# Split norm sums and gate, a reordered GDN chain and a smaller weight ring in the projection stage of a hybrid GDN / RWKV-7 block

## The chip, the cores and the metric

The kernel runs on one core of a Trainium2 chip. The metric is the device time of one launch in microseconds (us), lower is better. The five engines are named as in the profile: PE is TensorE, DVE is VectorE, ACT is ScalarE, POOL is GpSimd, SP is the queue that issues most DMAs.

## The reference

One layer on x of 512 tokens by 2048 features, all in fp32, with a memory of 256 tokens:

```python
xn = RMSNorm(h);  y = xn @ W_in            # columns for 8 GDN heads x 128 and 16 RWKV heads x 64
h += concat[GDN(y_gdn), RWKV7(y_rwkv)] @ W_out
h += CrossAttn(RMSNorm(h), RMSNorm(mem))   # 4 heads of 512 into the 256 memory tokens
h += SquaredReLU_MLP(RMSNorm(h))           # hidden 8192
out = RMSNorm_final(h)

# GDN, per head: q, k, v = silu(causal conv of 4 taps); z gates the output
q = l2norm(q) * 128 ** -0.5;  k = l2norm(k)
# per chunk: M = strict(kb k^T * gamma), solve (M + 1) [U, W] = [v*b, kb*exp(G)]
v_new = U - W @ S;  o = qd @ S + (q k^T * gamma) @ v_new;  S = S * exp(gl) + kt^T @ v_new
out = rmsnorm(o) * norm_w * silu(z)
# RWKV-7, per head: S_t = S_{t-1} (diag(w_t) + a_t b_t^T) + v_t k_t^T, o_t = S_t r_t,
# with a norm of the keys, a group norm of o over 64 channels, a bonus term (r*k summed) * v,
# and an output gate sigmoid(y_g1) @ g2 of rank 160
```

## The kernel before

Features lie on partitions and the 512 tokens on the free axis, so a product of one weight block is 128x128 times 128x512. Weights and activations are split into two f32r parts (hi and lo), and each product of fp32 operands is made as three: hi·hi, hi·lo and lo·hi. For weights a half tile of 128x1024 (512 KB) is read into a raw buffer `wraw`; ACT casts it to `whi`, DVE subtracts to get `wlo`. The raw ring has `NWR` = 3 buffers in the pool `pw`, `whi` and `wlo` have two each (`NWS`). A few products stay plain fp32, among them the sums over channels that the norms need (a product with a constant matrix: `ones`, or `bones`, which is ones in the two 64x64 blocks on the diagonal) and RWKV's output gate (`pgt`).

The program has two parts. The first, up to about 1211 us, is ordered by hand. Generators yield one operation at a time; `run()` estimates for each waiting operation when it could start, issues the earliest, and keeps a model clock of each engine. `TE`, `DV`, `AC`, `GS` and `SY` are the lanes of the engines and of SP; `SL` is SP with an added wait for what it stores. `after(...)` holds a generator until an event. All these operations have one line in the profile, L249. In this part run:

- `projections()`: 59 tiles py of the input projection (16 steps of 3 products each), then kp (keys of the memory, 16 tiles of two halves with 16 products each) and kq (32 halves of 24 products with 256 columns). For each head pair the tiles are r, k, v of RWKV and then q, k, v, z of one GDN head. `evict` and `qevict` take results out of PSUM into one of `NY` = 6 buffers `ybuf`; `qevict` then stores 256 KB to `KQd` (kqd) in DRAM.
- `loader()`: splits weight halves and refills the raw ring through `rawload`.
- `rwkv(j)` and `gdn(h)`, eight chains each: convolutions or token shifts, norms, products within the chunk, the inverse of a triangular matrix (`inverse_blocks` on GpSimd for 16x16 blocks, then levels on TensorE), and a scan over chunks (products `rs` and `gs`). Their results go to `mixd` (mx when read back).

In a GDN chain the three convolutions come first, then both norm sums (`gn`), then the products of keys with keys (`pkk`) and queries with keys (`pqk`), and then the inverse starts. Further norm sums are `gon` (output of GDN), and `pn`, `pb`, `pvr` (keys, bonus and group norm of RWKV). Temporaries of 128x512 come from small rings: `sr` (2), `st` (2), `sg` (3).

The second part is written in plain order; a tile framework sets its waits. It begins when the pools of the first part (`pm`, `pq`) are closed and a pool `pl` is opened in their place: the results in `mixd` are read back and split (`oh`, `ol`), vp makes the values of the memory from `wv` (line L125 for its products, L133/L134 for the split, L153 for the weight load), then vo, op, sc, at, up and dn follow. The pool `pw` with the raw ring stays open over both parts.

Of the kernel before, what the change touches and what calls it, by code (L numbers as in the profile page):

```python
# [27 lines left out]
for _n, _w in (("ident", 128), ("ones", 128), ("bones", 128), ("mA", 128),  # L28
               ("lv64", 2 * 64), ("cen", 64), ("sneg", 128), ("mbias", 128),
               ("rst64", 512)):  # L30
    CST[_n] = (_off, _w)
    _off += _w
# [13 lines left out]
def constants():  # L46
    c = np.zeros((P, NCST), np.float32)

    def put(name, a):
        o, w = CST[name]  # L50
        c[:, o:o + w] = a
# [4 lines left out]
    put("bones", (i[:, None] // 64 == i[None, :] // 64))  # L56
# [18 lines left out]
def build(tc, I, out):  # L75
# [9 lines left out]

    pq_cm = tc.tile_pool(name="pq", bufs=1)
# [22 lines left out]
    ident, ones, bones = K("ident"), K("ones"), K("bones")  # L109
# [30 lines left out]
    NWR, NWS, NY = 3, 2, 6  # L140
    wcnt = [0]

    def wraw():
        wcnt[0] += 1
        return tile_of(pw, [P, 1024], F32, "wraw", f"wraw{wcnt[0]}", NWR)
# [128 lines left out]
    def after(*ev):  # L274
        return lambda: ev in events
# [50 lines left out]

    def act_tile(nm, dt=F32R):
        return tile_of(pa, [P, 512], dt, "act", nm, 32)
# [16 lines left out]
    NSH = {"sr": 2, "st": 2, "sg": 3}  # L345
# [78 lines left out]
    dp = pq.tile([P, 149], F32, name="dp")  # L424
    omu = dp[:, 0:27]
    hw0, ha0, hka = dp[:, 27:35], dp[:, 35:43], dp[:, 43:51]
    hgnw = dp[:, 148:149]
    hconv = dp[:, 51:147]
    nA = dp[:, 147:148]

    def derived():
        yield DV.tensor_scalar(out=omu, in0=cols("mu"), scalar1=-1.0, scalar2=1.0, op0=ALU.mult, op1=ALU.add)
        for o, n in ((hw0, "w0"), (ha0, "a0"), (hka, "ka"), (hgnw, "gnw"), (hconv, "conv")):
            yield DV.tensor_scalar(out=o, in0=cols(n), scalar1=0.5, scalar2=None, op0=ALU.mult)
# [123 lines left out]
    sg1 = pq.tile([P, T], F32, name="sg1")  # L558
    y2 = pq.tile([P, T], F32, name="y2")
# [3 lines left out]
    def rows():  # L563
# [13 lines left out]
        yield AC.activation(wa[0:64, :], wa[0:64, :], AF.Tanh)  # L577
        yield from shiftmix(1, 1, sg1)
        yield AC.activation(sg1, sg1, AF.Tanh, scale=0.5)
        yield DV.tensor_scalar(out=sg1, in0=sg1, scalar1=0.5, scalar2=0.5, op0=ALU.mult, op1=ALU.add)  # L580
        events.add(("lowrank",))
# [5 lines left out]
        x_, e_ = short(t="st"), short(t="st")  # L587
# [11 lines left out]
        tail = short(t="st")  # L599
# [43 lines left out]
    def inverse_blocks(nm, store, m, tags, sh, out):  # L643
# [5 lines left out]
        s1, s2 = short(512, sh), short(512, sh)  # L649
        q = lambda a: a[0:np_].rearrange("p (a b) -> p a b", b=16)  # L650
        D, Td, Ud = q(s1[:, 0:256]), q(s1[:, 256:512]), q(s2[:, 0:256])
# [3 lines left out]
        for j in range(15):  # L655
            w = 15 - j
            t = s2[0:np_, 256:256 + w * (j + 1)].rearrange("p (a b) -> p a b", b=j + 1)
            yield GS.tensor_tensor(out=t, in0=D[:, j, j + 1:16].unsqueeze(2).broadcast_to([np_, w, j + 1]),
                                   in1=Td[:, j:j + 1, 0:j + 1].broadcast_to([np_, w, j + 1]), op=ALU.mult)
            yield GS.tensor_tensor(out=Td[:, j + 1:16, 0:j + 1], in0=Td[:, j + 1:16, 0:j + 1], in1=t, op=ALU.add)  # L660
        yield GS.tensor_copy(Ud, Td.rearrange("p a b -> p b a"))
        Tm, Tt = (tl(t)[:, 0:m * 32].rearrange("p (c t) -> p c t", t=64) for t in tags[1:])
# [40 lines left out]
    def rwkv(j):  # L703
        base = 3 + 7 * j
        js = slice(j * P, (j + 1) * P)
        lw, lg = tl("lw", P), tl("lg", 2 * P, 2)
        yield SY.dma_start(lw, I["w2a2"][:, js])
        yield SY.dma_start(lg[:, 0:P], I["g2a"][:, js])
        yield SY.dma_start(lg[0:32, P:2 * P], I["g2b"][:, js])
# [23 lines left out]
        yield TE.matmul(pn, bones, sq, start=True, stop=True)  # L733
# [44 lines left out]
        chain(inverse_blocks(f"ri{j}", store, 16, ("k", "r", "E2"), "sr", inv), 1, ("ri", j))  # L778
        yield DV.scalar_tensor_tensor(out=kp, in0=r_, scalar=col("rk", j), in1=kp, op0=ALU.mult, op1=ALU.mult)
        pb = psb(f"pb{j}")  # L780
        yield TE.matmul(pb, bones, kp, start=True, stop=True)
# [47 lines left out]
        yield AC.copy(ov, pov)  # L829
        yield after("ri", j)  # L830
# [13 lines left out]
        if j < 7:  # L844
            chain(rwkv(j + 1), 3)

# [27 lines left out]
        sq = short(t="st")  # L874
        yield AC.activation(sq, cen, AF.Square)
        pvr = psb(f"pvr{j}", "scr", 1)
        yield TE.matmul(pvr, bones, sq, start=True, stop=True)
# [11 lines left out]
    def gdn(h):  # L889
        base = 3 + 7 * h + 3  # L890
        gsh = lambda w=512: short(w, "sg")
        yield after("rows")
# [4 lines left out]
        silu = []  # L897
        for s in range(3):
            yield after("py", base + s)
            y = ybuf[ys[base + s]]  # L900
            a = gsh()
            cv = lambda i: hconv[:, (s * 8 + h) * 4 + i:(s * 8 + h) * 4 + i + 1]
            yield AC.activation(a, y[:, 0:512], AF.Copy, scale=cv(0))
            for i in range(1, 4):
                yield DV.scalar_tensor_tensor(out=a, in0=y[:, i:i + 512], scalar=cv(i), in1=a,
                                              op0=ALU.mult, op1=ALU.add)
            yfree.append(ys.pop(base + s))
            t = gsh()
            yield AC.activation(t, a, AF.Tanh)
            o = tl(("gq", "gk", "gv")[s])  # L910
            yield DV.scalar_tensor_tensor(out=o, in0=t, scalar=1.0, in1=a, op0=ALU.add, op1=ALU.mult)
            silu.append(o)
        q_, k_, v_ = silu
# [7 lines left out]

        c3 = lambda a: a.rearrange("p (c t) -> p c t", t=P)
        sqs = []
        for x in (k_, q_):
            sq = gsh()
            yield AC.activation(sq, x, AF.Square)
            pn = psb(f"gn{h}_{len(sqs)}", "mg")
            yield TE.matmul(pn, ones, sq, start=True, stop=True)
            sqs.append((sq, pn))
        for c in range(4):  # L930
            cs = slice(c * P, (c + 1) * P)
            if c == 0:
                EG = tl("gEG")
                yield AC.activation(EG, E, AF.Exp)
                eg = tl("eg", 4, 2)
                yield DV.tensor_copy(eg.unsqueeze(2), c3(EG)[:, :, P - 1:P])
            yield DV.scalar_tensor_tensor(out=E[:, cs], in0=E[:, cs], scalar=RT[:, c, 0, h:h + 1],
                                          in1=K("mbias"), op0=ALU.subtract, op1=ALU.min)
        yield AC.activation(E, E, AF.Exp)
        Es = tl("gEs")  # L940
        yield GS.tensor_tensor(out=c3(Es), in0=c3(E), in1=K("sneg").unsqueeze(1).broadcast_to([P, 4, P]), op=ALU.mult)
        nrm = []
        for (sq, pn), x, bias, tag in ((sqs[0], k_, None, "gkn"), (sqs[1], q_, b_lq, "gqn")):
            yield from rsq_(sq, pn, 1.0, b_eps6, bias)
            xn = tl(tag)
            yield DV.tensor_tensor(out=xn, in0=x, in1=sq, op=ALU.mult)
            nrm.append(xn)
        kn, qn = nrm
        kb = tl("gk")
        yield DV.tensor_tensor(out=kb, in0=kn, in1=B, op=ALU.mult)  # L950
        pkk = psb(f"pkk{h}", "mg")
        for c in range(4):
            cs = slice(c * P, (c + 1) * P)
            yield TE.matmul(pkk[:, cs], kn[:, cs], kb[:, cs], start=True, stop=True)
        wd, qd = tl("gq"), B
        yield DV.tensor_tensor(out=wd, in0=kb, in1=EG, op=ALU.mult)
        yield DV.tensor_tensor(out=qd, in0=qn, in1=EG, op=ALU.mult)
        NTm = tl("gEG")
        yield DV.tensor_tensor(out=NTm, in0=pkk, in1=Es, op=ALU.mult)

        def store(full):
            yield SY.dma_start(full[:, 0:4, :], c3(NTm)[hA, :, 0:64])
            yield SY.dma_start(full[:, 4:8, :], c3(NTm)[hB, :, 64:128])

        inv = []
        pqk = psb(f"pqk{h}", "mg")
        for c in range(4):
            cs = slice(c * P, (c + 1) * P)
            yield TE.matmul(pqk[:, cs], kn[:, cs], qn[:, cs], start=True, stop=True)
        pkt = psb(f"pkt{h}", "mg")  # L970
        for c in range(4):
            cs = slice(c * P, (c + 1) * P)
            yield TE.transpose(pkt[:, cs], kn[:, cs], ident)
        Aq = tl("gAq")
        yield DV.tensor_tensor(out=Aq, in0=pqk, in1=E, op=ALU.mult)
        chain(inverse_blocks(f"gi{h}", store, 8, ("gkn", "gk", "gqn"), "sg", inv), 1, ("gi", h))
        pvt = psb(f"pvt{h}", "mg")
        for c in range(4):
            cs = slice(c * P, (c + 1) * P)
            yield TE.transpose(pvt[:, cs], v_[:, cs], ident)  # L980
        vb, kt = tl("gv"), tl("gkt")
        yield DV.tensor_tensor(out=c3(kt), in0=c3(pkt), in1=RT[:, :, 2, h:h + 1].broadcast_to([P, 4, P]), op=ALU.mult)
# [386 lines left out]
```

## Time and profile before

| | |
|---|---|
| median of 3 runs | 3179.08 us (3178.40 to 3180.32) |
| profiled execution | 3178.97 us |
| its span in the profile | 3177.1 us |
| granted TensorE clock, mean | 0.997 |
| TensorE busy | 3127.4 us |
| DVE, ACT, POOL busy | 1527.5, 1153.6, 195.5 us |
| stages by start of their products | py from 10 us, kp from 994, kq from 1106, vp from 1211, up and dn from 1757 |

A row of the profile names line, engine and operation, then output <- inputs with buffer numbers left out, and the number of instructions. A plain fp32 product shows as two matmul records. The chain of waits is followed back from the last instruction; "issue" in it is time in which the engine waited for nothing that is recorded. Recorded durations of pipelined matmuls overlap, so what one costs TensorE is read from the distance between starts.

### The profile page before, as it was taken

Reading aid. Unit: us, or ns where it says so; the run is one execution under the profiler, and the core shown is the slowest. Engines: PE = TensorE matmul, PEld = TensorE weight load, DVE = VectorE, ACT = ScalarE, POOL = GpSimd, SP = SyncE. Lnnn points to the kernel's source line nnn. Section 1 sums busy time; section 2 is a strip of 40 time slices with the busy share of each in tenths; the row PEclk is TensorE's granted clock in tenths of the full one; section 3 lists DMA queues with packets and bytes.
Section 4 is the critical chain, followed back from the end, with each engine's and each line's share of the span. In section 5 each row is a group of like instructions: output and inputs, shape, how many; then the busy total and the mean of one; then the engine's idle time right before and its main releaser. Section 6 shows DMA issues by size and latency. Waiting matters only on the chain.

```text
span 3177.1 us, 44277 instructions
## 1 busy us (share of the span) xinstructions
PE 3127.4 (98%) x18294; PEld 2552.0 (80%) x18294; DVE 1527.5 (48%) x2157; ACT 1153.6 (36%) x1468; POOL 195.5 (6%) x549
## 2 busy tenths in 40 slices
PE   8999999999999999999999999999999999999997
PEld 6777777777778798878878888888888888888885
DVE  6555566565566646534336433333343333333344
ACT  5435344354355555543324322222221222222222
POOL 0121120220220200000000000000000000000000
PEclk9999999999999999999999999999999999999998
DMA  5322322322424577663323222222222223222222
GB/s 177 88 76 84 89 81 77 98 81 76 124 82 140 160 231 258 227 226 126 109 93 93 94 98 97 96 100 93 100 94 99 99 94 100 93 99 96 96 100 93
DMA packets 202363, 360.57 MB, mean 113 GB/s; under 512 B 88553, under 2 KB 107757, under 8 KB 202161
## 3 DMA queue, kind: packets, MB, share of 16 engines
q1 hardware_dynamic: 197552, 349.35, 34.7%
q10 hardware_dynamic: 4608, 8.39, 0.7%
q8 instruction: 144, 2.36, 0.3%
q14 instruction: 59, 0.48, 0.0%
HBM read 326.86 MB, written 30.81 MB: 113 GB/s over the span
## 4 chain that ended last, share of the span: by engine, by line
PE 95%; DMA 2%; ACT 1%; DVE 1%; issue 0%; SPq 0%; ACTq 0%; DVEq 0%
PE dn L125 22%; PE up L125 22%; PE py L249 21%; PE op L125 5%; PE sc L125 3%; PE kq L249 3%; PE at L125 3%; PE kp L249 2%; PE vo L125 2%; PE vp L125 2%; PE gs L249 1%; PE rs L249 1%; DMA mx<-mixd 1%; PE pgA L249 1%; PE po L249 0%; PE gn L249 0%
## 5 line engine op out<-in xcount | busy, mean ns | idle before, releaser
L133 ACT CAST whi<-wraw 128x1024 fp32r<-128x1024 f32 x368 | 387.1, 1052 | 1101.1 <-PE dn L125 471.3
L134 DVE TENSOR_TENSOR wlo<-wraw,whi 128x1024 fp32r<-128x1024 f32 x368 | 451.1, 1226 | 536.0 <-ACT whi L133 534.9
L125 PE MATMUL dn<-ul,whi 128*128 128x512 f32 x1024 | 399.3, 390 | 0.0
L125 PE MATMUL up<-nl,whi 128*128 128x512 f32 x1024 | 398.7, 389 | 0.0
L125 PE MATMUL dn<-uh,wlo 128*128 128x512 f32 x1024 | 398.4, 389 | 0.0
L125 PE MATMUL dn<-uh,whi 128*128 128x512 f32 x1024 | 398.4, 389 | 0.0
L125 PE MATMUL up<-nh,wlo 128*128 128x512 f32 x1024 | 398.3, 389 | 0.0
L125 PE MATMUL up<-nh,whi 128*128 128x512 f32 x1024 | 398.3, 389 | 0.0
L249 PE MATMUL py<-xhi,whi 128*128 128x512 f32 x928 | 377.2, 406 | 10.8 <-ACT xhi L249 10.3
L249 PE MATMUL py<-xlo,whi 128*128 128x512 f32 x928 | 379.2, 409 | 0.1
L249 PE MATMUL py<-xhi,wlo 128*128 128x512 f32 x928 | 375.1, 404 | 0.0
L249 DVE TENSOR_TENSOR wlo<-wraw,whi 128x1024 fp32r<-128x1024 f32 x180 | 221.3, 1230 | 145.8 <-ACT whi L249 135.6
L249 ACT CAST whi<-wraw 128x1024 fp32r<-128x1024 f32 x180 | 188.9, 1049 | 271.9 <-PE py L249 215.4
L1263 DVE TENSOR_TENSOR h<-h,dn 128x512 f32<-128x512 f32 x128 | 88.1, 688 | 400.1 <-PE dn L125 400.1
L125 PEld LDWEIGHTS dn<-ul,whi 128*128 128x128 f32 x1024 | 192.2, 188 | 42.6 <-DVE ul L134 2.9
L125 PEld LDWEIGHTS up<-nh,wlo 128*128 128x128 f32 x1024 | 192.2, 188 | 40.3 <-issue 0.2
L125 PEld LDWEIGHTS up<-nl,whi 128*128 128x128 f32 x1024 | 192.2, 188 | 40.1 <-issue 0.2
L125 PEld LDWEIGHTS dn<-uh,wlo 128*128 128x128 f32 x1024 | 192.2, 188 | 40.0
L125 PEld LDWEIGHTS dn<-uh,whi 128*128 128x128 f32 x1024 | 192.2, 188 | 39.7
L125 PEld LDWEIGHTS up<-nh,whi 128*128 128x128 f32 x1024 | 192.2, 188 | 39.7
L249 PEld LDWEIGHTS py<-xhi,whi 128*128 128x128 f32 x928 | 175.4, 189 | 52.7 <-ACT xhi L249 10.3
L249 PEld LDWEIGHTS py<-xlo,whi 128*128 128x128 f32 x928 | 175.3, 189 | 41.4 <-issue 5.8
(558 smaller groups left out, 4710.2 us busy)
## 6 DMA issues: line engine op xcount, KB each, us to landing
wraw<-in_w_up SPq DMA_DIRECT2D x128, 512.0 KB, 3.5
wraw<-in_w_dn SPq DMA_DIRECT2D x128, 512.0 KB, 3.6
wraw<-in_w_in SPq DMA_DIRECT2D x118, 512.0 KB, 3.8
wraw<-in_wk SPq DMA_DIRECT2D x32, 512.0 KB, 3.8
wraw<-in_wqT SPq DMA_DIRECT2D x32, 512.0 KB, 4.2
wraw<-in_wv SPq DMA_DIRECT2D x32, 512.0 KB, 3.7
wraw<-in_wo SPq DMA_DIRECT2D x32, 512.0 KB, 4.2
wraw<-in_w_out SPq DMA_DIRECT2D x32, 512.0 KB, 3.7
```

The lines of the kernel that those rows point to most:

```text
L125: PE.matmul(o, l, r, start=start, stop=stop)
L133: S.copy(hi, src)
L134: V.tensor_tensor(out=lo, in0=src, in1=hi.bitcast(F32), op=ALU.subtract)
L249: f(*a, **k)
L1263: V.tensor_tensor(out=hres[n], in0=hres[n], in1=pt, op=ALU.add)
```

## The change

- GDN chain: the key's convolution comes first, then its norm, `pkk`, and the start of the inverse with temporaries of its own (`sgi`, `sgj`; the matrix in `gN`); then query, value and z. The inverse's last steps wait for the event `gq`. The columns of W_in are laid out as k, q, v, z for this.
- `sums_`: each of the 48 norm sums first splits its operand (`sumh`, `suml`, one pair for all, guarded by a lock) and makes two f32r products with a constant in f32r.
- Gate: `sg1`, `y2` and the gate weights are split (`sgh`, `sgl`, `sst`, `lgs`), four f32r products (the last of 96 rows) in place of two fp32 ones; the gate weights are loaded later in the chain.
- `NY` is 4; the rings `st` and `sg` are 1 and 2; some temporaries are other tiles now.
- In the first part the raw ring has 2 buffers, in a pool `pr` that is closed with the others; in the second it has 3, in `pl`. The third load at the start goes.
- `bones` and the f32r constants are made on chip; some halved parameters are halved in place.

```diff
-    NWR, NWS, NY = 3, 2, 6
+    NWS, NY = 2, 4
+    raw_pool, NWR = pr, 2
...
+    def sums_(pt, which, sq):
+        yield lambda: not lock
+        lock.append(pt)
+        hi, lo = (tile_of(pm, [P, 512], F32R, t, f"{t}_{pt.tensor.name}", 1) for t in ("sumh", "suml"))
+        yield from split_(sq, hi, lo)
+        yield TE.matmul(pt, which, hi, start=True, stop=False)
+        yield TE.matmul(pt, which, lo, start=False, stop=True)
+        lock.pop()
...
-    NSH = {"sr": 2, "st": 2, "sg": 3}
+    NSH = {"sr": 2, "st": 1, "sg": 2}
...
-        yield TE.matmul(pn, bones, sq, start=True, stop=True)
+        yield from sums_(pn, bonesr, sq)
...
-        yield TE.matmul(pg, lg[:, 0:P], sg1, start=True, stop=False)
-        yield TE.matmul(pg, lg[0:32, P:2 * P], y2[0:32, :], start=False, stop=True)
+        gh, gl, gs = lgs[:, 0:P], lgs[:, 2 * P:3 * P], lgs[0:96, P:2 * P]
+        for n, (l, r) in enumerate(((gh, sgh), (gh, sgl), (gl, sgh), (gs, sst[0:96]))):
+            yield TE.matmul(pg, l, r, start=n == 0, stop=n == 3)
...
+        k_ = yield from conv(0, 1, "gk")
...
+        kn = yield from normed(k_, None, "gkn", 0)
...
+        NTm = tl("gN")
+        yield DV.tensor_tensor(out=NTm, in0=pkk, in1=Es, op=ALU.mult)
...
+        chain(inverse_blocks(f"gi{h}", store, 8, ("gkn", "gk", "gqn"), lambda: (tl("sgi"), tl("sgj", 240)),
+                             after("gq", h), inv), 1, ("gi", h))
+        q_ = yield from conv(1, 0, "gq")
+        qn = yield from normed(q_, b_lq, "gqn", 1)
...
+        v_ = yield from conv(2, 2, "gv")
...
-    issue(rawload(2))
...
     pm_cm.__exit__(None, None, None)
     pq_cm.__exit__(None, None, None)
+    pr_cm.__exit__(None, None, None)
     pl = es.enter_context(tc.tile_pool(name="pl", bufs=1, reuse_waits="tile"))
+    raw_pool, NWR = pl, 3
```

More of the change, by code (lines that the diff above doesn't have):

```diff
@@ L27 @@
 _off = 0
[L28 removed]
+for _n, _w in (("ident", 128), ("ones", 128), ("mA", 128),
                ("lv64", 2 * 64), ("cen", 64), ("sneg", 128), ("mbias", 128),
@@ L641, in views, with inverse_blocks @@
         return full, blk
-    def inverse_blocks(nm, store, m, tags, sh, out):
+    def inverse_blocks(nm, store, m, tags, temps, ready, out):
         np_ = 4 * m
@@ L777, in rwkv @@
         inv = []
-        chain(inverse_blocks(f"ri{j}", store, 16, ("k", "r", "E2"), "sr", inv), 1, ("ri", j))
+        chain(inverse_blocks(f"ri{j}", store, 16, ("k", "r", "E2"), lambda: (short(), short(240)), lambda: True, inv),
+              1, ("ri", j))
         yield DV.scalar_tensor_tensor(out=kp, in0=r_, scalar=col("rk", j), in1=kp, op0=ALU.mult, op1=ALU.mult)
         pb = psb(f"pb{j}")
-        yield TE.matmul(pb, bones, kp, start=True, stop=True)
+        yield from sums_(pb, bonesr, kp)
         bon = tl("bon")
@@ L829, in rwkv @@
         yield AC.copy(ov, pov)
+        lg = tl("lg", 2 * P)
+        yield SL.dma_start(lg[:, 0:P], I["g2a"][:, js])
+        for r in range(3):
+            yield SL.dma_start(lg[r * 32:r * 32 + 32, P:2 * P], I["g2b"][:, js])
         yield after("ri", j)
@@ L891, in gdn, with conv, normed @@
         gsh = lambda w=512: short(w, "sg")
+        c3 = lambda a: a.rearrange("p (c t) -> p c t", t=P)
+        def conv(i, s, tag):
+            yield after("py", base + i)
+            y = ybuf[ys[base + i]]
+            a = tl(tag)
+            cv = lambda i: hconv[:, (s * 8 + h) * 4 + i:(s * 8 + h) * 4 + i + 1]
+            yield AC.activation(a, y[:, 0:512], AF.Copy, scale=cv(0))
+            for n in range(1, 4):
+                yield DV.scalar_tensor_tensor(out=a, in0=y[:, n:n + 512], scalar=cv(n), in1=a,
+                                              op0=ALU.mult, op1=ALU.add)
+            yfree.append(ys.pop(base + i))
+            t = gsh()
+            yield AC.activation(t, a, AF.Tanh)
+            yield DV.scalar_tensor_tensor(out=a, in0=t, scalar=1.0, in1=a, op0=ALU.add, op1=ALU.mult)
+            return a
+        def normed(x, bias, tag, nm):
+            sq = gsh()
+            yield AC.activation(sq, x, AF.Square)
+            pn = psb(f"gn{h}_{nm}", "mg")
+            yield from sums_(pn, onesr, sq)
+            yield from rsq_(sq, pn, 1.0, b_eps6, bias)
+            xn = tl(tag)
+            yield DV.tensor_tensor(out=xn, in0=x, in1=sq, op=ALU.mult)
+            return xn
         yield after("rows")
@@ L913, in gdn @@
-        q_, k_, v_ = silu
+        k_ = yield from conv(0, 1, "gk")
+        EG = tl("gEG")
+        yield AC.activation(EG, E, AF.Exp)
+        eg = tl("eg", 4, 2)
+        yield DV.tensor_copy(eg.unsqueeze(2), c3(EG)[:, :, P - 1:P])
+        for c in range(4):
+            cs = slice(c * P, (c + 1) * P)
+            yield DV.scalar_tensor_tensor(out=E[:, cs], in0=E[:, cs], scalar=RT[:, c, 0, h:h + 1],
+                                          in1=K("mbias"), op0=ALU.subtract, op1=ALU.min)
+        yield AC.activation(E, E, AF.Exp)
@@ new lines, in gdn @@
+        Es = tl("gEs")
+        yield GS.tensor_tensor(out=c3(Es), in0=c3(E), in1=K("sneg").unsqueeze(1).broadcast_to([P, 4, P]), op=ALU.mult)
+        kn = yield from normed(k_, None, "gkn", 0)
+        kb = tl("gk")
+        yield DV.tensor_tensor(out=kb, in0=kn, in1=B, op=ALU.mult)
+        pkk = psb(f"pkk{h}", "mg")
+        for c in range(4):
+            cs = slice(c * P, (c + 1) * P)
+            yield TE.matmul(pkk[:, cs], kn[:, cs], kb[:, cs], start=True, stop=True)
+        NTm = tl("gN")
@@ new lines, in gdn @@
+        wd, qd = tl("gq"), B
+        yield DV.tensor_tensor(out=wd, in0=kb, in1=EG, op=ALU.mult)
+        yield DV.tensor_tensor(out=qd, in0=qn, in1=EG, op=ALU.mult)
+        pqk = psb(f"pqk{h}", "mg")
+        for c in range(4):
+            cs = slice(c * P, (c + 1) * P)
+            yield TE.matmul(pqk[:, cs], kn[:, cs], qn[:, cs], start=True, stop=True)
+        Aq = tl("gAq")
+        yield DV.tensor_tensor(out=Aq, in0=pqk, in1=E, op=ALU.mult)
+        pkt = psb(f"pkt{h}", "mg")
+        for c in range(4):
+            cs = slice(c * P, (c + 1) * P)
+            yield TE.transpose(pkt[:, cs], kn[:, cs], ident)
@@ new lines, in gdn @@
+        kt = tl("gkt")
+        yield DV.tensor_tensor(out=c3(kt), in0=c3(pkt), in1=RT[:, :, 2, h:h + 1].broadcast_to([P, 4, P]), op=ALU.mult)
+        events.add(("gq", h))
+        v_ = yield from conv(2, 2, "gv")
+        pvt = psb(f"pvt{h}", "mg")
+        for c in range(4):
+            cs = slice(c * P, (c + 1) * P)
+            yield TE.transpose(pvt[:, cs], v_[:, cs], ident)
+        vb = tl("gv")
+        yield DV.tensor_tensor(out=c3(vb), in0=c3(pvt), in1=RT[:, :, 1, h:h + 1].broadcast_to([P, 4, P]), op=ALU.mult)
@@ L920, in gdn @@
         yfree.append(ys.pop(base + 3))
[L922 to L982, printed above, removed]
@@ L1032, in gdn @@
         pn = psb(f"gon{h}", "scg", 1)
-        yield TE.matmul(pn, ones, sq, start=True, stop=True)
+        yield from sums_(pn, onesr, sq)
         yield from rsq_(sq, pn, 1.0 / 128, b_eps6)
         yield DV.tensor_tensor(out=o, in0=o, in1=sq, op=ALU.mult)
-        ot = gsh()
-        yield DV.scalar_tensor_tensor(out=ot, in0=o, scalar=hgnw, in1=zs, op0=ALU.mult, op1=ALU.mult)
-        yield SL.dma_start(mixd[h], ot)
+        yield DV.scalar_tensor_tensor(out=o, in0=o, scalar=hgnw, in1=zs, op0=ALU.mult, op1=ALU.mult)
+        yield SL.dma_start(mixd[h], o)
         if h < 7:
@@ L1192, in build @@
             cnt[0] += 1
-            raw = pw.tile([P, 1024], F32, tag="wraw", name=f"kqr{cnt[0]}", bufs=NWR)
+            raw = pl.tile([P, 1024], F32, tag="wraw", name=f"kqr{cnt[0]}", bufs=NWR)
             for i in range(2):
```

87 lines of the change are left out of this document (45 added, 42 removed).

## The prediction

> **What bounds the kernel now.** I read the head of the page first (span, busy shares, the chain of waits by engine), then the table of what TensorE waited for, once for the whole span and once for 100 to 1030 us, the stretch of projections and recurrent chains after the start.
>
> ```profile
> span 3177.1 us, 44277 instructions
> PE 3127.4 (98%) x18294; PEld 2552.0 (80%) x18294; DVE 1527.5 (48%) x2157; ACT 1153.6 (36%) x1468; POOL 195.5 (6%) x549
> PE 95%; DMA 2%; ACT 1%; DVE 1%; issue 0%; SPq 0%; ACTq 0%; DVEq 0%
> ...
> PE py L249 <- ACT xhi L249: 11.2, 2, 10.3
> PE vp L125 <- DVE wlo L134: 3.1, 3, 1.5
> PE kq L249 <- DVE wlo L249: 1.2, 1, 1.2
> ```
>
> ```profile
> PE gi2u L249 <- DVE gkn L249: 0.2, 1, 0.2
> PE gi3u L249 <- DVE gkn L249: 0.2, 1, 0.2
> PE gi4u L249 <- DVE gkn L249: 0.2, 1, 0.2
> ```
>
> The first fence is of the whole span, the second is the full answer for 100 to 1030 us. TensorE is the bound: 98% busy, 95% of the chain, and in those 930 us it waited 0.6. TensorE time taken out of that stretch comes off the span, and time put in is added. It waits today at the start (11.2 for the input), in kq (1.2) and in vp (3.1). Three runs lie from 3178.40 to 3180.32, and 0.2% (6.4 us) is about what a measurement of this kernel can tell from no change. The sum is made against the profiled execution: 3178.97 us, 1.9 of it outside the span, and 0.1 below the median of 3179.08.
>
> **Products in two parts.** By the order of the changed program's instructions 48 fp32 sums (gn 16, and 8 each of gon, pn, pb, pvr) become 96 f32r products, and 16 fp32 gate products (pgt) become 32. Pieces of the chain (start, us, what), then TensorE's timeline around one sum and around a 64-row group:
>
> ```profile
> 2499.95 42.39 PE up L125 x187
> 147.42 1.91 PE gn L249 x4
> 185.92 1.91 PE pgt L249 x4
> ...
> 555.89 0.39 PE L249 MATMUL py<-xhi,whi 128*128 128x512 f32 x1
> 556.12 1.02 PE L249 MATMUL pn<-sr,cst 128*128 128x512 f32 x2
> 556.58 0.80 PE L249 MATMUL py<-xlo,whi 128*128 128x512 f32 x1
> 557.22 0.40 PE L249 MATMUL py<-xhi,wlo 128*128 128x512 f32 x1
> ...
> 155.30 0.81 PE L249 MATMUL pu<-tA,E 64*64 64x64 f32 x22
> 156.04 0.50 PE L249 MATMUL py<-xlo,whi 128*128 128x512 f32 x1
> 156.38 0.40 PE L249 MATMUL py<-xhi,wlo 128*128 128x512 f32 x1
> 156.61 0.40 PE L249 MATMUL py<-xhi,whi 128*128 128x512 f32 x1
> ...
> 159.45 1.12 PE L249 MATMUL pA<-wa,lw 64*128 64x512 f32 x2
> 160.50 0.43 PE L249 MATMUL rs<-BK,BTz 128*128 128x64 f32 x2
> ```
>
> An f32r product of 512 columns takes 42.39/187 = 0.227 us of the engine. One fp32 sum is recorded as two matmuls: from 556.12 to 557.22 lie 1.10 us, less one py product of 0.227 leaves 0.87; two in a row (gn, four records) take 1.91, 0.955 each. I take 0.91. Sums: 48 × 0.91 = 43.7 less 96 × 0.227 = 21.8, so −21.9 (−20.0 by 0.87, −24.0 by 0.955). Gate: 8 pairs at 1.91 = 15.3, less 32 × 0.227 = 7.3, so −8.0 (−7 if the 96-row product pays a change of shape that its 32-row forerunner didn't).
>
> TensorE changes between 64 and 128 rows 368 times by the new order, 342 before. A py product behind a 64-row group takes 0.34 (156.04 to 156.38) against 0.23 for the next, +0.11; a 64-row fp32 product between 128-row ones takes 1.05 (159.45 to 160.50) against 0.87, +0.18. At 0.15 each, 26 changes are +3.9 (2.9 to 4.7). TensorE work together: −26.0 (−29 to −22).
>
> **What the split costs elsewhere.** Each sum now needs an ACT copy and a DVE subtract of 128x512, and the single pair sumh/suml with its lock lets one sum through at a time.
>
> ```profile
> 1219.39 0.62 ACT L133 CAST oh<-mx 128x512 fp32r<-128x512 f32 x1 [1.20 <-DMA mx<-mixd]
> 1220.04 0.69 DVE L134 TENSOR_TENSOR ol<-mx,oh 128x512 fp32r<-128x512 f32 x1 [0.59 <-ACT oh L133]
> ```
>
> 48 × 0.62 = 30 us of ACT and 48 × 0.69 = 33 of DVE, on engines that are 36 and 48% busy, hidden as long as TensorE has projection matmuls queued ahead. In the new order at least 1.25 us of such work stands between each split step and its product, more than either step takes. The GDN reorder and the sums shift others closer: of some 104 waits of the RWKV state products (rs) 39 have under 0.7 us of TensorE work ahead of them, 20 before; of the 80 of GDN's (gs) 25 instead of 68. The one shortfall grows by 4 us and the other shrinks by 11; in the profile 20 such rs waits cost nothing that is recorded. I put in +2 (−3 to +9). Of the y buffers I expect nothing: before a product needs an eviction the next tile's 48 products (10.9 us) are always queued, in both orders.
>
> GDN's new order, its own tiles and the constants now made on chip move no TensorE work: nothing. 16 more small g2b loads add 16 issues to SP, some 0.33 us each (as the queue's rows below), ahead of weight loads that have 5 us to spare in the projections: nothing. The third weight load goes from the start, the g2 loads come later there.
>
> ```profile
> 5.34 0.59 SPq L249 DMA_DIRECT2D wraw<-in_w_in  x1
> wraw<-in_w_in SPq DMA_DIRECT2D x6, 512.0 KB, 5.2
> wraw<-in_wk SPq DMA_DIRECT2D x25, 512.0 KB, 3.5
> ```
>
> The issue at 5.34 leaves the queue ahead of input that TensorE waits for; loads there land in 5.2 us (10 to 42 us), in the quiet early kp in 3.5 (last line). A gain is bounded by the difference, 1.7, a loss by about the same again should the second load come late: −1 (−3 to +3).
>
> **Raw ring of two.** This is the price I find largest. ACT casts whi from a raw buffer, DVE subtracts wlo, then SP refills that buffer. ACT, DVE and SP in one half tile of kq, then landings at a slower pace (window 1125 to 1137: first and last of its four loads, and the median landing), then a load and the cast that waited for its landing at full pace:
>
> ```profile
> 1159.68 1.05 ACT L249 CAST whi<-wraw 128x1024 fp32r<-128x1024 f32 x1
> 1160.76 1.23 DVE L249 TENSOR_TENSOR wlo<-wraw,whi 128x1024 fp32r<-128x1024 f32 x1 [1.67 <-ACT whi L249]
> 1162.01 0.33 SPq L249 DMA_DIRECT2D wraw<-in_wqT  x1
> 1162.56 1.05 ACT L249 CAST whi<-wraw 128x1024 fp32r<-128x1024 f32 x1
> ...
> 1125.91 0.33 SPq L249 DMA_DIRECT2D wraw<-in_wqT  x1
> 1136.71 0.33 SPq L249 DMA_DIRECT2D wraw<-in_wqT  x1
> wraw<-in_wqT SPq DMA_DIRECT2D x4, 512.0 KB, 4.1
> ...
> 1208.26 0.33 SPq L153 DMA_DIRECT2D wraw<-in_wv  x1
> 1214.22 1.05 ACT L133 CAST whi<-wraw 128x1024 fp32r<-128x1024 f32 x1 [1.58 <-DMA wraw<-in_wv]
> ```
>
> From cast to refill are 2.33 us (1159.68 to 1162.01), then the landing L; a half takes 2.88 (1159.68 to 1162.56). With three buffers the cycle 2.33 + L may last 8.65, so L up to 6.3 hides. With two it may last 5.77: L over 3.4 is paid, and the half takes (2.33 + L)/2. L depends on the pace: 4.1 when halves come every 3.6 us (1125.91 to 1136.71, three steps), 5.96 at 2.88 (1208.26 to 1214.22). On a straight line between the two, pace and landing agree at a half of 3.43 with L = 4.5: +0.54. In the new order GDN's last chain ends by kp10 (before: in kq), so all 32 halves of kq run bare: 32 × 0.54 = +17.4. With L = 4.1 it is 3.215 and +10.6; with 5.96, 4.145 and +40.4. The 12 bare halves of kp have no stores beside them (3.5 lands: 2.92 a half): +1. In the projections a half lasts 24 × 0.227 = 5.4 us, two of them 10.9, and L up to 8.5 hides.
>
> The Trainium skill, "SBUF — State Buffer", section "The DMA setup-cost knee", gives a transfer as a fixed 2 us or so plus its bytes at 436 GB/s. By that, an estimate, 512 KB land in 3.2 us, a ring of two could turn in 2.77, and this term would be nought. The trace's 3.5 in quiet, 4.1 and 5.96 speak against it.
>
> **From kq to vp.** Today five wv loads are issued during kq, behind one another on SP. The new raw buffers of vp lie in a pool that opens after the manual part, and SP's new order is: last KQd store, mx0, mx1 (which waits for that store to land), mx2, first wv load, mx3 to mx5 (each waits for the split of an earlier mx), second wv load. Everything behind mx1 waits with it, and ACT casts whi in the same order, behind the oh copies.
>
> ```profile
> 1212.67 3.99 DMA kqd<-y
> 1216.68 1.27 SPq L1108 DMA_DIRECT2D mx<-mixd  x3
> ...
> wraw<-in_wv SPq DMA_DIRECT2D x12, 512.0 KB, 4.9
> mx<-mixd SPq DMA_DIRECT2D x16, 256.0 KB, 4.2
> ```
>
> The last two rows are medians of 1211 to 1250 us. Counted from kq's last matmul: copy of y about 0.6 (as oh), store landed 4.0 later at 4.6, mx1 and mx2 issued at 0.42 each, first wv at about 5.2, landed 10.1, whi 1.05: TensorE starts at 11 and waits some 0.8 more for wlo. The half ends at 14.7. mx2, issued at 4.9, lands at 9.1, its copy and subtract (0.62, 0.69) end near 10.4; mx5, then the second weight at 10.8, landed at 15.7, whi and wlo to 18.0: 3.3 idle. Later weights come in pairs and I see no further wait. 11 + 0.8 + 3.3 = 15.1, less the 3.1 of today: +12.0 (+8 if store and loads land in the 3.5 of the quiet stretch, +17 if five later halves lose a us each).
>
> **Sum.** −26.0 + 2 − 1 + 17.4 + 1 + 12.0 = +5.4, so 3184.4 us.
>
> **Rivals.** Forecast (0.50): the ring binds in kq with L of 4.1 to 4.9 and vp starts late: 3177 to 3193.
>
> Two buffers suffice (0.22): the loads of kq land in 3.4 or less once fewer are outstanding. Then the terms +17.4 and +1 go: 3184.4 − 18.4 = 3166.0, faster. For it: 3.5 in quiet. Against: a store of 256 KB goes out beside every load of kq, and 4.1 was seen even at the slower pace. It decides at L = 3.4. The page named above gives 3.2 for a load and so this outcome.
>
> Landing stays at 5.96 (0.15): the store's and the next load's bytes meet whatever the pace. 40.4 instead of 17.4: 3207. Against it: 4.1 at 3.6 us a half.
>
> The chains wait (0.13): the 19 further rs waits with little work ahead each cost a DVE step, 19 × 0.69 = 13 instead of 2: 3195. For it: one 128x512 step is longer than their cover. Against: the 20 that are there today show no wait.
>
> **Chances and range.** Of the forecast's span 0.27 lies within 0.2% (3172.7 to 3185.4) and 0.23 above; rival one is 0.20 faster and 0.02 within; the other two, 0.28, are slower. Faster 0.20, same 0.29, slower 0.51. The range 3166 to 3200 leaves out most of the 5.96 case and the tail of the first rival.
>
> **What would show it.** Right: the sums as two records of 0.23 each and py tiles shorter; kq's cast-to-cast at 3.2 to 3.6 us with ACT's wait put to the landing of wqT; an idle TensorE of 9 to 12 us between kq and vp. Wrong: kq still at 2.88 a half (then 3166), waits of rs or of a sum's product in 100 to 1030 us, or wv loads issued ahead of kq's end.

## The result and the profile after

The changed kernel takes 3195.60 us in the median of four runs (3191.53 to 3197.52), against 3179.05 (3178.40 to 3180.32) before: slower by 16.5 us, ratio 1.005 with a 95% interval of 1.0032 to 1.0067. The forecast was 3184.4 with a range of 3166 to 3200: the direction and the two largest places were right, the size was a third of what came. The profiled execution took 3194.72 us, span 3192.9. Head of the page, then what TensorE waited for (whole span):

```profile
span 3192.9 us, 44395 instructions
PE 3114.7 (98%) x18294; PEld 2557.4 (80%) x18294; DVE 1564.1 (49%) x2227; ACT 1188.8 (37%) x1532; POOL 196.7 (6%) x547
PE 88%; DMA 5%; DVE 2%; ACT 2%; POOL 1%; issue 1%; SPq 0%; ACTq 0%; DVEq 0%; POOLq 0%
...
PE vp L126 <- ACT whi L134: 10.3, 1, 10.3
PE kq L251 <- DVE wlo L251: 7.7, 21, 0.7
...
```

TensorE is busy for 12.7 us less than before (3127.4) and the span is 15.8 longer: work left TensorE and waits came. The share of TensorE in the chain fell from 95 to 88%, DMA's rose from 2 to 5. Of the waits shown, the first is for the late vp weights and the second is the ring in kq (1.2 before). The other waits for wlo rose little: 3.7 in vp and 3.6 in kp, where the kernel before had 3.1 and 2.4. New are waits of the chains, in the same window in which the kernel before was looked at, 100 to 1030 us:

```profile
PE pW L251 <- DMA lw<-in_w2a: 3.7, 5, 1.1
PE pwt L251 <- DVE E L251: 2.3, 1, 2.3
PE pv L251 <- ACT Kt L251: 1.7, 1, 1.7
PE rs L251 <- DVE Qs L251: 1.6, 3, 1.3
PE kp L251 <- DVE wlo L251: 1.3, 1, 1.3
PE gn L251 <- DVE suml_gn L251: 0.7, 1, 0.7
PE pat L251 <- ACT Kt L251: 0.7, 1, 0.7
PE pkB L251 <- DVE bon L251: 0.5, 1, 0.5
```

Without the row of kp that is 11.2 us of the chains, where the kernel before had 0.6. The split sum itself, on TensorE's timeline, and the gate in the chain:

```profile
80.62 0.40 PE L251 MATMUL py<-xlo,whi 128*128 128x512 f32 x1
80.86 0.39 PE L251 MATMUL pn<-sumh_pn,bonesr 128*128 128x512 f32 x1
81.09 0.39 PE L251 MATMUL py<-xhi,wlo 128*128 128x512 f32 x1
81.32 0.40 PE L251 MATMUL pn<-suml_pn,bonesr 128*128 128x512 f32 x1
81.56 0.39 PE L251 MATMUL py<-xhi,whi 128*128 128x512 f32 x1
...
197.18 0.95 PE pgt L251 x4
```

Starts stand 0.23 to 0.24 us apart, sums and py products alike: 96 x 0.235 = 22.6 for the sums, 21.1 less than the 43.7 of before. A gate takes 0.95 where it took 1.91: 7.7 less over eight. Three casts of kq on ACT, the median landing from 1140 to 1200 us, and the passage to vp:

```profile
1180.69 1.05 ACT L251 CAST whi<-wraw 128x1024 fp32r<-128x1024 f32 x1 [0.65 <-DMA wraw<-in_wqT]
1184.40 1.05 ACT L251 CAST whi<-wraw 128x1024 fp32r<-128x1024 f32 x1 [1.48 <-DMA wraw<-in_wqT]
1187.61 1.05 ACT L251 CAST whi<-wraw 128x1024 fp32r<-128x1024 f32 x1 [1.04 <-DMA wraw<-in_wqT]
wraw<-in_wqT SPq DMA_DIRECT2D x17, 512.0 KB, 4.4
...
1214.09 2.61 SPq L1146 DMA_DIRECT2D mx<-mixd  x3
1216.79 0.38 SPq L155 DMA_DIRECT2D wraw<-in_wv  x1
...
1222.19 1.04 ACT L134 CAST whi<-wraw 128x1024 fp32r<-128x1024 f32 x1 [2.25 <-DMA wraw<-in_wv]
1223.29 0.80 PE L126 MATMUL vp<-mhl,whi 128*128 128x512 f32 x1 [10.26 <-ACT whi L134]
```

The casts come 3.71 and 3.21 apart and each waits for its load, as foretold; the loads land in 4.4. vp's first weight goes out at 1216.79, behind the mx loads, and its cast ends 10.2 us after TensorE went idle. What the forecast did not have shows in windows of four microseconds (TensorE's busy time is the second figure; the granted clock is the column ahead of the last two):

```profile
824.00:828.00 4.00, 1.63 (x51) 1.05 (x53) 2.58 (x4) 3.96 (x7) 0.76 (x3) 1.00 0.51 127
828.00:832.00 4.00, 4.00 (x67) 2.86 (x58) 2.58 (x7) 2.78 (x6) 3.34 (x9) 0.57 0.68 198
...
988.00:992.00 4.00, 2.71 (x45) 2.43 (x42) 3.84 (x5) 3.59 (x7) 0.57 (x1) 0.56 0.39 126
992.00:996.00 4.00, 4.00 (x17) 3.48 (x16) 1.90 (x4) 0.03 (x1) 0.00 (x0) 0.59 0.80 246
...
1221.00:1225.00 4.00, 1.25 (x3) 0.74 (x4) 1.73 (x2) 2.18 (x3) 0.00 (x0) 0.50 0.87 276
1225.00:1229.00 4.00, 3.68 (x15) 2.90 (x14) 1.46 (x4) 1.67 (x2) 0.00 (x0) 0.70 0.91 314
```

Behind these idle times the granted clock falls to 0.5 to 0.7 for some microseconds. TensorE's busy time, times the share of the clock that is missing, is 1.7, 1.2, 1.6, 0.6 and 1.1 in the five rows below 1.00: 6.3 us lost to slow work (an estimate from these rows). In the kernel before no window between the start and the last microseconds shows less than 0.98.

### The profile page after: what moved, and what is told of

Its sections match the earlier page's. It is cut to its first block, busy times and chain, and to the rows that moved or that the text cites. A ratio compares the mean times of both kernels' runs of the same rounds, so it can differ in the third digit from the quotient of the medians.

```text
span 3192.9 us, 44395 instructions
## 1 busy us (share of the span) xinstructions
PE 3114.7 (98%) x18294; PEld 2557.4 (80%) x18294; DVE 1564.1 (49%) x2227; ACT 1188.8 (37%) x1532; POOL 196.7 (6%) x547
## 4 chain that ended last, share of the span: by engine, by line
PE 88%; DMA 5%; DVE 2%; ACT 2%; POOL 1%; issue 1%; SPq 0%; ACTq 0%; DVEq 0%; POOLq 0%
PE dn L126 22%; PE up L126 22%; PE py L251 19%; PE op L126 5%; PE sc L126 3%; PE at L126 3%; PE vo L126 3%; PE vp L126 2%; DMA wraw<-in_wqT 2%; PE kp L251 1%; DVE wlo L251 1%; ACT whi L251 1%; DMA wraw<-in_wk 1%; PE rs L251 1%; PE gs L251 1%
## 5 line engine op out<-in xcount | busy, mean ns | idle before, releaser
L251 PEld LDWEIGHTS py<-xhi,wlo 128*128 128x128 f32 x928 | 175.4, 189 | 36.4 <-DVE wlo L251 1.1
```

The lines of the kernel that those rows point to most:

```text
L251: f(*a, **k)
```

## Experiments

Times are medians; those of the first four stand against 3179.75 of the kernel before on the same chip, the next four (b_ring to a_vpact) against 3179.43, b_idle against 3180.22, and a_vpw2, a_oldgdn and b_idle1 against 3179.74. In the text `pl`, which is opened after the first part, is called the late pool.

**a_vpw.** The two raw buffers of the first part in the pool that stays open:

```diff
-    raw_pool, NWR = pr, 2
+    raw_pool, NWR = pw, 2
...
+        if raw_pool is None and wcnt[0] % 3 == 2:
+            return tile_of(pl, [P, 1024], F32, "wraw3", f"wraw{wcnt[0]}", 1)
+        return tile_of(pw, [P, 1024], F32, "wraw", f"wraw{wcnt[0]}", 2)
```

> The changed kernel with one edit: its two raw buffers of the first part lie in the pool that stays open, and the third of the second part in the late pool, so that vp's first two weight loads can be issued while kq runs. Theory (late weights cost about 12 us between kq and vp, of which two prefetched halves give back most): 3195.6 - 10 to 13, 3183 to 3186 us, TensorE's wait of 10.3 us ahead of vp gone, kq still near 3.35 us a half. Rival (the time is lost to bytes, so loads moved ahead only slow kq's own): 3192 to 3196, kq longer by what vp gains.

Measured 3188.78 (3187.20 to 3192.00), 6.8 less than the changed kernel, neither as the theory nor as the rival had it. The wait ahead of vp was still there:

```profile
1212.44 0.38 SPq L157 DMA_DIRECT2D wraw<-in_wv  x1
1218.51 0.79 PE L126 MATMUL vp<-mhl,whi 128*128 128x512 f32 x1 [10.07 <-ACT whi L134]
```

a_vpact and a_vpw2 below say why. The 6.8 came in small parts elsewhere: from 42 to 1350 us the recorded idle time of TensorE is 30 us, 37 in the changed kernel, spread over the chains, kq and vp.

**a_r3.** A ring of three in the first part, the late pool as in the changed kernel. To make room, two small weight tiles and a temporary of the inverse use tiles that are idle then, and the gate z waits for the inverse's store (`gst`):

```diff
-    raw_pool, NWR = pr, 2
+    raw_pool, NWR = pr, 3
+    issue(rawload(2))
-        lg = tl("lg", 2 * P)
+        lg = tl("kp")[:, 0:2 * P]
-        lw = tl("lw", P)
+        lw = tl("E1", shape=[P, 8, 65]).rearrange("p a b -> p (a b)")[:, 0:P]
-        chain(inverse_blocks(f"gi{h}", store, 8, ("gkn", "gk", "gqn"), lambda: (tl("sgi"), tl("sgj", 240)),
+        chain(inverse_blocks(f"gi{h}", store, 8, ("gkn", "gk", "gqn"), lambda: (tl("gz"), tl("sgj", 240)),
...
+        yield after("gst", f"gi{h}")
         zs = tl("gz")
```

> The changed kernel with a raw ring of three in the first part (room made by letting two small weight tiles and one GDN temporary use tiles that are idle then); vp's weights are as late as in the changed kernel. Theory (kq is paced by the refill of two buffers): kq back at 2.89 us a half, 15 us less, and the 10.3 us ahead of vp stay: 3178 to 3182; if the new waits in kp come from the ring too, 3174. Rival (kq is paced by the stores or by bytes): kq at 3.2 or more a half, 3189 to 3196.

Measured 3168.94 (3165.80 to 3174.93): 26.7 less, more than the theory's 15 to 21. The kq products of the changed kernel, then of this one (first to last start):

```profile
L251 PE MATMUL kq<-khi,whi x256: 277/283/283, 1105.6 to 1212.5; 128*128 128x256 f32 x128
```

```profile
L251 PE MATMUL kq<-khi,whi x256: 278/283/290, 1100.1 to 1193.3; 128*128 128x256 f32 x128
```

106.9 became 93.2 us, 13.7 less, with the same stores and bytes beside it, and the 21 waits of kq are down to one of 0.7: the refill paced kq. Another 4.8 went from kp (from its first product to kq's, 126.0 to 121.2). The profiled execution of this kernel was the slowest of its six (3174.93), so its stages add up to 19.8 of the 26.7 only; where the other 7 lie isn't traced. The tile moves, and the order of the chains that came with them, are in the 26.7 too: the ring of three was not tried without them.

**a_pw3.** The same ring of three in `pw` over both parts (`raw_pool, NWR = pw, 3`, and no change of pool later), with the tile moves of a_r3.

> The same with the ring of three in the pool that stays open over both parts, as in the kernel before: both waits should go. Theory: the two add up, 3195.6 - 15 - 13 = 3167 us, up to 5 less if kp's waits go with the ring; then the split products' saving of 26 us shows, less 7 of waits of the chains. Rival (the reordered chains cost more than the products save): 3176 to 3182.

Measured 3156.91 (3155.40 to 3161.80), ratio 0.9926 (0.991 to 0.9943): 12.0 less than a_r3, 38.7 less than the changed kernel and 22.8 less than the kernel before. It is the fastest of all that ran; the theory put it 10 higher, since it gave the ring 12 too little. In the traced pair vp's first product comes 8.3 us earlier than in a_r3, and vp's products then span 4.7 less.

**a_pw3lw.** lw for the next chain is loaded with the gate weights:

```diff
+        if j < 7:
+            lwn = e1()
+            yield SY.dma_start(lwn, I["w2a2"][:, js.stop:js.stop + P])
-            chain(rwkv(j + 1), 3)
+            chain(rwkv(j + 1, lwn), 3)
```

> As the run before, and the next RWKV chain's small weight tile lw is loaded with the gate weights of the chain ahead, before the SP queue stands behind GDN's inverse. Theory: pW's waits for that load (3.7 us in all) go, 3 to 4 us less than the run before. Rival (other work of the chain is late then as well): within 1 us of it.

Measured 3162.40 (3159.73 to 3165.28): 5.5 more, not 3 to 4 less. The two longest kinds of TensorE's waits from 42 to 1105 us:

```profile
PE kp L251 <- DVE wlo L251: 3.0, 2, 1.9
PE kp L251 <- DVE y L251: 2.6, 1, 2.6
...
```

pW's waits are gone, and all waits of this window are 7.1 us, 10.3 in a_pw3: the theory's 3 us did come. They were lost again. At the seam from py to kp the clock is 0.57 to 0.84 in three of four windows from 980 to 996 us, 1.00 in a_pw3, and over the whole trace slow work costs 6.8 us, 3.4 there. By the order of its matmuls TensorE changes its row size 385 times, 364 there, which is 3 us at the forecast's 0.15. Every edit gives the planner another order; that this is the rest is not shown.

**b_ring.** The kernel before with the changed kernel's ring and pools only (`raw_pool, NWR = pr, 2`, later `pl, 3`, no third load).

> The kernel before with the ring alone as in the changed kernel: two raw buffers in a pool of the first part, three in the late pool, no third load at the start; sums, gate and GDN order as before. Theory (the price hangs on how many halves of kq run without chain work beside them; here GDN's last chain still lies in the first 11): 21 x 0.46 = 10 in kq, 12 to 15 between kq and vp, few us of lower clock behind the idle time: 3201 to 3208. Rival (the ring costs what it cost with the reordered chain, 3195.6 - 3156.9 = 38.7): 3216 to 3219.

Measured 3206.28 (3203.51 to 3209.66): 26.9 more, as the theory said and well under the 38.7 of the reordered kernel. Waits from 1100 to 1330 us:

```profile
PE vp L127 <- ACT whi L135: 8.2, 1, 8.2
PE kq L252 <- DVE wlo L252: 4.8, 11, 1.2
...
```

The same ring costs more where GDN's last chain has left kq. kq's products (first to last start) span 114.2 us here and 104.2 in the kernel before, 10.0 more as the theory had it; between a_pw3 (92.2) and the changed kernel (106.9) it is 14.7. That is 4.7 of the 11.8 between the two prices. The rest isn't separated; waits that come with both the ring and the new order are under "Why the prediction was right or wrong".

**a_f32sum.** a_pw3 (its tile moves too) with `yield TE.matmul(pt, which.bitcast(F32), sq, start=True, stop=True)` as the whole of `sums_`.

> The changed kernel with the ring of three in the open pool (a_pw3) and its 48 norm sums in fp32 again; the gate stays split. Theory (the saving of 48 x 0.91 - 96 x 0.227 = 21.9 us comes through whole): 3178.8, at 3176 to 3181. Rival (the splits' ACT and DVE steps and the lock make waits that eat part of it): 3165 to 3173.

Measured 3186.42 (3185.32 to 3189.18), 29.5 more than a_pw3: more than the whole saving. It is not the products alone: by the order of its instructions TensorE changes its row size 398 times, 364 in a_pw3, and 34 changes at the forecast's 0.15 are 5 us of the 7.6 that go beyond the saving. No run changes that count alone.

**a_reord.** The gate in fp32 too, so that the GDN order, the smaller rings and the tile moves of a_pw3 are left.

> As a_f32sum, and the gate in fp32 too: what is left of the change is the order of the GDN chain and the smaller rings of temporaries and y. Theory (the new order brings the 7 us of chain waits that the changed kernel shows): 3185 to 3188, slower than before. Rival (those waits come from the splits; the order is free): 3177 to 3181.

Measured 3190.09 (3186.93 to 3192.04), 10.7 over the kernel before: the theory's side, though dearer. Its trace has 7.7 us of waits from 42 to 980 us, as the theory had it, but 6.4 of them are of products of the inverse (ri1u to ri5u); pW's are 1.3, and those of pv and pat are gone. By the order of its instructions there are 394 row changes, 342 before (52 x 0.15 = 8 us). The gate is worth 3.7 between these two runs, 7.7 on the timeline; each run has another order too, and the two were not separated.

**a_vpact.** a_vpw, with vp's first two halves loaded and split ahead of the loop that reads mx.

> a_vpw with vp's first two weight halves loaded and split in the program ahead of the loop that reads mx back. In a_vpw both loads had been issued during kq and TensorE still sat 10.1 us, with ACT's cast of the first weight behind three copies that wait for mx. Theory (the place in ACT's order holds vp back, not the load): 8 to 11 us less than a_vpw, 3178 to 3181. Rival (the loads themselves or the pool's waits hold it): 3186 to 3190.

Measured 3188.09 (3185.51 to 3191.79), like a_vpw, though the wait ahead of vp is 7.5 in its trace, 10.1 there: ACT's place in the queue was not what held vp back, that theory fell. The trace showed the cause: vp's first half had drawn the late pool's buffer, and the two loads seen in kq were for its second and third.

**a_vpw2.** a_vpw with `wcnt[0] % 3 == 1`, so that the late pool's buffer is the third half's.

> a_vpw with the buffers counted so that vp's first two weight halves take the two raw buffers of the open pool (in a_vpw the very first took the late pool's buffer, so its load went out only after kq). Theory (the late first load makes the 10 us ahead of vp and the low clock behind it): the idle time ahead of vp under 2 us, 8 to 12 less than a_vpw: 3177 to 3181. Rival (ACT's order behind the mx copies or kq's bytes hold vp back even so): 3185 to 3190.

Measured 3184.17 (3182.59 to 3190.99), 4.6 under a_vpw and 11.4 under the changed kernel. vp now follows kq at once, and the wait stands two weight halves later:

```profile
1211.78 0.43 SPq L157 DMA_DIRECT2D wraw<-in_wv  x1
1219.20 0.79 PE L126 MATMUL vp<-mhl,whi 128*128 128x512 f32 x1 [6.14 <-ACT whi L134]
```

So both were half right: the late first load made the 10 us, and the third load, behind the mx reads, makes 6.1 of its own. This run shows the cause of the 10 us; the theory's time came out 3 us too low.

**a_oldgdn.** a_pw3 with the GDN chain in its old order (and `sg` of three).

> a_pw3 (split sums and gate, ring of three in the open pool) with the GDN chain in its old order: q, k, v convolutions first, both norms together, inverse after pqk and pkt, temporaries of the inverse from the ring sg of three; W_in's columns as before. Theory (the reorder costs by itself: more row changes on TensorE, 364 against 347, lw late behind the inverse on SP): 3 to 8 less than a_pw3's 3156.9, 3149 to 3154. Rival (the reorder earns its keep once the sums are split): 3160 to 3168.

Measured 3298.24 (3294.61 to 3299.86), 141 more than a_pw3. I had expected less. Waits of the whole span, without the start's:

```profile
PE py L251 <- DVE y L251: 21.9, 3, 7.3
...
PE gon L251 <- ACT sumh_gon L251: 8.1, 4, 2.0
PE kp L251 <- DVE y L251: 7.3, 1, 7.3
```

Four waits of 7.3 us are for an eviction into a y buffer. In the code a GDN chain starts when the last has ended, and until then q, k, v and z of its head sit in y: four, which is all that there are now. So the new order and `NY` = 4 belong together. The y buffers were not tried alone, nor is it shown how much of the 141 is theirs: the recorded waits are 82 us from 42 to 1130 (8.8 of them gon's for the one pair sumh/suml), and the clock stood at 0.5 for long stretches behind them, by some 54 us of slow work. Row changes are 347 here, so they are not what made it slow.

**b_idle.** The kernel before with seven waits put in:

```diff
+            if n % 7 == 5 and n > 5:
+                yield DV.tensor_reduce(out=zz, in_=prev, op=ALU.max, axis=mybir.AxisListType.X)
+                yield TE.matmul(pt[:, 0:1], ones, zz, start=True, stop=True)
```

> The kernel before with seven short waits put in: ahead of seven projection tiles (one in each block) a DVE maximum over the tile just finished, and a product of one column that needs it (its result is overwritten). Nothing else changes. Theory (a wait costs its own length, some 0.7 of DVE plus 0.3 to 0.6 of queue and hand-over): 7 x 1.0 to 1.3, so 3186 to 3188, granted clock 1.00 throughout. Rival (behind a wait of about a microsecond the granted clock falls to 0.5 to 0.7 for some 4 us, as in the changed kernel's windows): up to 2 us more for each wait that it follows, 3190 to 3202, with low-clock stretches right behind the waits.

Measured 3233.83 (3232.83 to 3234.56): 53.6 more. Six waits are recorded, of 3.5 us, since DVE had other work queued ahead of the maximum. TensorE behind one of them, then the clock in windows of 3.4 us:

```profile
439.13 0.39 PE L249 MATMUL py<-xhi,wlo 128*128 128x512 f32 x1
442.99 0.59 PE L249 MATMUL py<-zz,cst 128*128 128x1 f32 x2 [3.46 <-DVE zz L249]
...
444.01 0.63 PE L249 MATMUL py<-xlo,whi 128*128 128x512 f32 x1
444.43 0.63 PE L249 MATMUL py<-xhi,wlo 128*128 128x512 f32 x1
```

```profile
441.60:445.00 3.40, 2.02 (x6) 1.73 (x7) 2.42 (x5) 2.00 (x2) 2.85 (x8) 0.50 0.51 153
445.00:448.40 3.40, 3.40 (x8) 1.98 (x7) 0.00 (x0) 1.58 (x2) 1.64 (x6) 0.50 0.17 21
448.40:451.80 3.40, 3.40 (x17) 2.80 (x16) 1.41 (x2) 1.64 (x3) 0.00 (x0) 0.99 0.09 19
```

A product takes 0.42 us for some 5 us behind this wait (444.01 to 444.43), 0.23 before and after. All six waits had a stretch at half clock. The waits are 21.1 us and the slow work 14.9 by the clock, 36 of the 53.6. The edit also gave the chains another order: by the order of its matmuls TensorE changes its row size 416 times, 342 in the kernel before, and 74 at the forecast's 0.15 are 11 us more. That part is an estimate.

**b_idle1.** The same with `AC.copy(zz, prev[:, 0:1])` for the maximum.

> b_idle with the seven waits made shorter: ACT copies one column of the tile just finished in place of DVE's maximum. In b_idle a wait was 3.5 us, TensorE ran at half clock for some 5 us behind each, and the kernel lost 7.7 us a wait. Theory (the clock falls only behind waits of about 2 us and more; here they are 0.5 to 1.5): 7 x 1 = 7, 3184 to 3190, few stretches of low clock. Rival (any wait of half a microsecond brings it): 7 x 3.5, 3200 to 3206.

Measured 3208.72 (3207.65 to 3210.30): 29.0 more, between theory and rival, 4.1 a wait. Six waits are 1.6 us and one is 1.0, and the clock fell behind two of the six. Here behind one that brought it, and one that did not:

```profile
438.00:442.00 4.00, 3.49 (x12) 2.78 (x13) 3.01 (x4) 2.46 (x4) 3.45 (x8) 0.77 0.36 131
...
564.00:568.00 4.00, 3.61 (x15) 2.70 (x16) 2.86 (x4) 2.49 (x5) 3.51 (x7) 1.00 0.30 91
```

The waits, 10.5 us, and 3.4 of slow work are 14. The other 15 go with another order of the chains: gs holds TensorE for 23.8 us by the distance between starts, 17.7 in the kernel before, pgA 5.0 for 1.5, pb 7.0 for 4.1. TensorE changes its row size 406 times, 342 before; 64 at 0.15 are 10 us. So the waits alone cost about 2 us each here, not 4.1, and neither theory nor rival had what cost the rest.

## Why the prediction was right or wrong

- **Products in two parts: right.** −21.9 and −8.0 were forecast, the timeline shows −21.1 and −7.7. Repeating the products in fp32 (a_f32sum) gave more, 29.5, but there the order changed too.
- **Row changes: not tested alone.** 26 at 0.15 were put in for the change. The runs whose order of matmuls has many more (394 to 416: a_reord, a_f32sum, b_idle and b_idle1) are all slower than their products, waits and clock explain, by some 4 to 16 us where 0.15 a change gives 5 to 11. That speaks for the term; no run changes the count alone.
- **Raw ring in kq: right.** +17.4 was forecast with L = 4.5 and 3.43 us a half; measured are L = 4.4 and 106.9 us for the 32 halves, 3.34 each, 13.7 more than with three buffers. By the SBUF page's fit (Trainium skill, "SBUF — State Buffer", section "The DMA setup-cost knee") a load would take 3.2, an estimate, and two buffers would do. That does not hold here: the loads of kq, with a store beside each, land in 4.4.
- **The ring elsewhere: a path was left out.** I gave kp +1 and the rest nothing. The memory's tiles (`in_memT`) pass through the raw ring as well, and ACT works on them between copies of the chains. In the changed kernel (ACT, then the product that waited for its copy):

```profile
817.52 1.06 ACT L251 ACTIVATE wraw<-wraw 128x1024 f32<-128x1024 f32 x1 [1.15 <-DMA wraw<-in_memT]
824.59 1.06 ACT L251 ACTIVATE wraw<-wraw 128x1024 f32<-128x1024 f32 x1
825.67 0.58 ACT L251 COPY Kt<-pkA 64x512 f32<-64x512 f32 x1
826.30 0.33 PE L251 MATMUL pv<-cst,v 64*64 64x64 f32 x4 [1.68 <-ACT Kt L251]
```

The waits of pv, pat and pwt, and rs waits over 1 us, are in all four traces with the new GDN order and two raw buffers (the changed kernel, a_vpw, a_vpact, a_vpw2). They are in none of the five with that order and three (a_r3, a_pw3, a_pw3lw, a_f32sum, a_reord), nor in b_ring with two and the old order. So they go with the two together, though the runs with three also have the tile moves (and a_oldgdn, which waits almost everywhere, has pwt's too). The step from the ring to each wait is read from the rows above and is not shown by a run.

- **From kq to vp: right, with some luck in the number.** +12.0 was forecast, and between a_r3 and a_pw3 lie 12.0. But the wait is 10.3 in the changed kernel and 8.2 in a_r3 where I had 11, and the slow clock behind it was not in the sum. The reason given (the weights' place behind mx on SP) held in a_vpw2, in two steps.
- **Chain waits: the step that failed.** "I put in +2 (−3 to +9)": the trace has 11.2 us of them, 0.6 before. I looked for them at rs and gs, by counting work ahead of each. rs has 1.6 and a sum's product (gn) 0.7, which the forecast named as a sign that it is wrong. The most came at pW (3.7), whose lw load stands behind the inverse's stores on SP, and at pwt, pv, pat and pkB (5.2). The order showed pW's queue; I had followed only the SP entries of the weights and of mx.
- **The clock: missing.** 6.3 us of slow work behind idle time are in no term of the sum. Every term that made TensorE wait was priced at its length.
- **Rivals.** That two buffers suffice is refuted (a_r3). That landing stays at 5.96 too (4.4). The rival in which the chains wait came to 3195, almost what was measured, but by 13 us of rs waits; rs waited 1.6, so the agreement is luck.

By runs, the 16.5 are the ring of two 26.7, the late pool 12.0 and everything else −22.8 (a_pw3 against the kernel before), where the forecast had 18.4, 12.0 and −25.0; the three add up to 15.9, since the kernel before stood at 3179.75 beside these runs. The ring takes 8.3 of the missing 11.1, and the rest of the change 2.2. By the traces, as an estimate, the chains' waits are 8.6 above what was put in and the slow clock 6.3, the products gave 1.1 less, and kq and vp cost 3.7 and 1.1 less than forecast: 11.2 together. Both accounts agree where the ring's surplus is part of the chains' waits and of the low clock behind them.

## What to carry to other kernels

Where one engine bounds a kernel, price a buffer taken away by the full cycle of its slot (cast, subtract, issue, landing at the pace in question) in each stage that has no other work to hide it, for everything that passes through the ring, and remember that moving such work away uncovers the stage. A wait of the bounding engine costs more than its length when its clock follows: keep a table of idle time and granted clock in small windows beside each other. If a pool opens late, ask where in each queue its first loads will stand; a_pw3 kept the savings of this change, with the ring of three in the pool that stays open, and ran at 0.9926 (0.991 to 0.9943) of the kernel before.

## What the runs showed of the hardware that was not expected

The granted clock of TensorE follows short waits: behind each of six waits of 3.5 us it stood at 0.5 for 3.4 or 6.8 us (b_idle), behind waits of 1.6 us in two cases of six (b_idle1), and products that take 0.23 us then took 0.42. The Trainium skill, "TensorE: Matmul & The Clock Gate", section "HAM oscillation — how this bites in real kernels", asks for no idle gap of more than some 3.4 us. The waits of 3.5 agree with it; those of 1.6 show that shorter ones can bring the low clock as well.

The low stretches come in steps. Ahead of the last microseconds those of the changed kernel, b_idle and b_idle1 last 3.41, 6.83 or 10.24 us, one, two or three times 3.413. In b_idle the starts of the six lie 126.29, 129.71, 129.71, 129.71 and 133.12 us apart, which is 37, 38, 38, 38 and 39 times the same step (by the granted clock in its trace). So where a wait falls between two steps may matter beside its length. That is not the whole of it: two waits of 1.58 us in b_idle1 lay each within one step, and one brought the low clock and the other did not.
